# Gating sixteen modulation pieces on the gMLP's gated products

## The chip, the cores and the metric

The kernel runs as one program on one NeuronCore of a Trainium2 chip. The metric is the device time of one execution in microseconds (us), as the median of several runs. The engines are TensorE (PE, matmuls), VectorE (DVE), ScalarE (ACT), GpSimd (POOL) and SyncE (SP), which here issues DMAs.

## What is computed

Two trunk layers over 512 latent tokens of width 1024 with 256 context tokens, one sample, fp32. Layer 0 mixes tokens by windowed attention, layer 1 by a chunked gMLP; a routed mixture of experts (MoE) with 16 experts, two per token, follows each. Around every mixer stands a modulation that is computed from the conditioning vector. Cut to what matters here (layer 1):

```python
mod_l = silu(c) @ w_mod[i] + b_mod[i]          # six rows of 1024: shift, scale, gate of mixer and of MoE
hl = x * (1 + sc_a) + sh_a
z = gelu(hl @ w_in + b_in); u, v = z[..., :1024], z[..., 1024:]
v = layer_norm(v, ln_g, ln_b)                  # over the width
s = einsum("gpq,bnqgc->bnpgc", w_s, v) + b_s   # chunks of 128 tokens, 8 groups of 128 columns
yl = (u * s) @ w_out
x = layer_norm(ALPHA * x + g_a * yl, ln1_g, ln1_b)
hl = x * (1 + sc_f) + sh_f                     # input of the router and the experts
x = layer_norm(ALPHA * x + g_f * moe(hl), ln2_g, ln2_b)
```

## The kernel before

**Modulation pieces.** Layer 1's product `silu(c) @ w_mod[1]` is computed without TensorE. `w_mod` comes from HBM in pieces `("mt", 1, j)`, j from 0 to 47, each a 128x1024 tile holding 128 outputs on its partitions. `gemt(1, j)` multiplies such a tile by the broadcast row `srow[0]` (the activated c, stored in HBM as `sdr`) and sums along the row into one column of `mv[1]`. For the pieces 32 to 47 an odd j is done by VectorE in one instruction (line 361, product and sum), an even j by GpSimd (line 363, the product, in place) and ScalarE (line 364, the sum). After every eighth j small VectorE steps (lines 370, 372) finish eight columns, and for some a TensorE transpose and a DMA write them out as a row. The columns 24 to 47 are wanted by the router's matrices (lines 761 to 777 in `ln1_rows`) and by the second MoE.

**The weight stream.** All weight tiles stand in one list, `pieces`, in the order in which SyncE issues their DMAs into the buffers `raw`. `adv(...)` marks a piece as used and lets the stream run on: `LR[0]` loads and `LS[0]` splits ahead of it. A split (lines 226, 227) turns a weight tile into a high part `wh` on ScalarE and the remainder `wl` on VectorE, so that fp32 products are made of three matmuls in a faster format: high by high, low by high, high by low.

**The gMLP.** It comes after layer 0's MoE. First v is projected for four token tiles (`vhalf`), its statistics taken (line 646, 651) and it is normalised (`vnorm`: a chain of small VectorE steps `cny`, `cnv`, `cnu`, lines 734 to 746, the mean term `cnm` at line 656, and then ScalarE at line 1360). The last of the four tiles has its statistics only when the u loop starts. The u loop (`for f in range(8)`) is the place of the change. One iteration f projects u for 128 columns over all tokens (24 matmuls, lines 1399 to 1401, of which the third is the first that needs `wl`), runs `gemt` for two pieces, applies gelu to u on ScalarE (`uT`, line 1406), makes the gate matmuls (line 1409, eight instructions, two per token tile of v), and on VectorE scales and adds the bias (`sg`, line 1412) and multiplies by `uT` (1415). The product is split for the output projection: ScalarE casts the high half (1417), VectorE subtracts it (1418, the low half, `gp[:, 1]`, which the change names `lo`). `mix_out(1, "wout", ...)` then multiplies all eight gated tiles by `wout` (lines 792 to 794), with the small router matmuls of lines 768 and 771 between.

**What sets the order.** The Python code issues instructions to a Tile scheduler, which simulates a timeline and fixes each engine's instruction order; waits go by semaphores. Code order, dependencies and buffer counts therefore all bear on where an instruction stands on its engine, and each engine runs its list strictly in order.

Of the kernel before, what the change touches and what calls it, by code (L numbers as in the profile page):

```python
# [8 lines left out]
F32 = mybir.dt.float32  # L9
# [4 lines left out]
OP = mybir.AluOpType  # L14
# [87 lines left out]
def hybrid_kernel(ctx: ExitStack, tc: tile.TileContext, A, out):  # L102
    nc = tc.nc
    V, SC, PE, GP, SP = nc.vector, nc.scalar, nc.tensor, nc.gpsimd, nc.sync
# [14 lines left out]
    def slot(shape, dt=F32, nm="s"):  # L119
        return S.tile(shape, dt, name=f"{nm}{nid()}", tag="s")  # L120
# [7 lines left out]
    def hslot(shape, dt=F32, nm="h"):  # L128
        return PP[0].tile(shape, dt, name=f"{nm}{nid()}", tag="h")
# [7 lines left out]
    def psB():  # L137
        return ps.tile([128, 512], F32, name=f"pb{nid()}", tag="B", bufs=2)

    def psT(dt=F32):  # L140
        return ps.tile([128, 512], dt, name=f"pt{nid()}", tag="T", bufs=2)

    def small(shape, dt=F32, nm="m", bufs=2):
        return sm.tile(shape, dt, name=f"{nm}_{nid()}", tag=nm, bufs=bufs)

    def tt2(shape, dt=F32, nm="t"):
        return sm.tile(shape, dt, name=f"{nm}_{nid()}", tag="t2", bufs=9)
# [3 lines left out]
    pieces = [("mod", 0, j) for j in range(16)]  # L151
# [10 lines left out]
    def moe_pieces(l):  # L162

        r, us = [], UNITS[l]

        def use(v, js):
            r.extend(p for p in [("moe", l, v, j) for j in js] if p not in r)
        for i, (v, o, n, row) in enumerate(us):
            use(v, range(8))
            if i:  # L170
                use(us[i - 1][0], range(8, 12))
            if i == 1:
                use(v, range(8, 12))
        use(us[-1][0], range(8, 12))
        return r

    pieces += moe_pieces(0)
    pieces += [("winv", j) for j in range(8)] + [("ws",)]
    for j in range(8):
        pieces += [("winu", j), ("mt", 1, 32 + 2 * j), ("mt", 1, 33 + 2 * j)]  # L180
    pieces += [("wout", j) for j in range(8)]
    pieces += moe_pieces(1)
    pos = {p: i for i, p in enumerate(pieces)}
# [3 lines left out]
    LS, LR = [4], [8]  # L187
# [57 lines left out]
    def raw(*p):  # L245
        i = pos[p]
        used.add(i)
        issue(i + 1)
        return raws[p]

    def hl(*p):
        ensure_split(pos[p] + 1)
        return pairs[p]

    def adv(*p):
        i = pos[p]
        issue(i + 1 + LR[0])
        ensure_split(i + 1 + LS[0])
        issue(i + 1 + LS[0] + LR[0])
# [55 lines left out]
    sdr = dr.tile([1, D], F32, name="sdr")  # L315
# [10 lines left out]
    mv = [cst.tile([128, 48], F32, name=f"mv{l}") for l in range(2)]  # L326
# [28 lines left out]
        if n >= 2:  # L355
            V.tensor_scalar(m, m, 1.0, None, op0=OP.add)

    def gemt(l, j):
        w = raw("mt", l, j)
        if (j % 4 != 3 if l and j < 32 else j % 2):  # L360
            V.scalar_tensor_tensor(w, w, 1.0, srow[0], op0=OP.mult, op1=OP.mult, accum_out=mv[l][:, j:j + 1])  # L361
        else:
            GP.tensor_mul(w, w, srow[0])  # L363
            SC.activation(w, w, AF.Identity, accum_out=mv[l][:, j:j + 1])
        adv("mt", l, j)
        if j % 8 < 7:
            return
        i = j // 8
        m = mv[l][:, i * 8:i * 8 + 8]
        V.tensor_add(m, m, bcol[:, l, i * 8:i * 8 + 8])  # L370
        if i in (1, 4):
            V.tensor_scalar(m, m, 1.0, None, op0=OP.add)
        if i >= 2:
            q = psT()
            PE.transpose(q[0:8, 0:128], m, idf)
            r = tt2([8, 128], F32, "gr")
            SC.copy(r, q[0:8, 0:128])
            SC.dma_start(mdr[l * 4 + i - 2].rearrange("(a b) -> a b", b=128), r)

    def load_row(ap, nm="row", alloc=slot, q=SC):  # L380
        t = alloc([128, D], F32, nm)
        q.dma_start(t, ap.to_broadcast([128, D]))
        return t

    LS[0], LR[0] = 4, 14
    srow = []
# [18 lines left out]
    for a in range(2):  # L405
        cr = raw("cT", a)
        hi, lo = slot([128, 4, 256], F32R, "cTh"), slot([128, 4, 256], F32R, "cTl")
# [6 lines left out]
    for a in range(4):  # L414
        xr = raw("xT", a)
        hi, lo = hslot([128, 2, 512], F32R, "hTh"), hslot([128, 2, 512], F32R, "hTl")
# [158 lines left out]
    def after(i, b, c=mybir.DependencyClass.NoSync):  # L575
        tc.add_manual_dep(i.ins, b.ins.name, mybir.DependencyInfo(
            c, mybir.DependencyReason.DATA), reason="order")
# [71 lines left out]
    def ln_rstd(st, w):  # L649
        mv = small([128, 2], F32, w + "mv")  # L650
        V.bn_aggr(mv, st)
        v = small([128, 3], F32, w + "nv")
        V.tensor_scalar(v[:, 0:1], mv[:, 1:2], EPS, None, op0=OP.add)
        y = newton([v[:, i:i + 1] for i in range(3)], w)
        nmr = small([128, 1], F32, w + "nm")
        V.scalar_tensor_tensor(nmr, mv[:, 0:1], -1.0, y, op0=OP.mult, op1=OP.mult)
        return y, nmr
# [607 lines left out]
    def mix_out(l, name, X, lh):  # L1265
        ga, g1, b1 = ln1_rows(l)
        for j in range(8):
            hl(name, j)
        LS[0], LR[0] = 0, 8
        s = small([128, 4, 16], F32, "rs", 1)  # L1270
        lg = psB()[:, 0:64]
        st = small([128, 4, 2, 6], F32, "ast", 1)
        for n in range(2):
            for t in range(4):
                f = out_half(l, name, n, lh, X[t], ga, t, lg)
                V.bn_stats(st[:, t, n, :], X[t][:, n * 512:(n + 1) * 512])
                f()
                if n:
                    x = X[t]
                    rstd, nmr = ln_rstd(st[:, t], "a")  # L1280

                    def sig(t=t, rstd=rstd, nmr=nmr):
                        R = RT[l]
                        u = small([128, 16], F32, "ru")
                        V.scalar_tensor_tensor(u, R["se"], nmr, R["be"], op0=OP.mult, op1=OP.add)
                        V.scalar_tensor_tensor(u, lg[:, t * 16:(t + 1) * 16], rstd, u, op0=OP.mult, op1=OP.add)
                        return SC.activation(s[:, t, :], u, AF.Sigmoid)
                    with tc.issue_after(sig().ins):
                        SC.activation(x, x, AF.Identity, bias=nmr, scale=rstd)
                        SC.dma_start(hdr[t * 128:(t + 1) * 128, :], x)  # L1290
            adv(name, 4 * n + 3)
        issue(pos["moe", l, 2, 0])
        RT[l]["s"] = s
        route(l, s)

        def rest(t0, t1):
            for t in range(t0, t1):
                V.tensor_mul(X[t], X[t], g1)
                V.tensor_add(X[t], X[t], b1)
        return rest  # L1300
# [4 lines left out]
    rest = mix_out(0, "wo", X0, lambda t, c, s: OT[t, c // 4][:, s, (c % 4) * 128:(c % 4 + 1) * 128])  # L1305
    py, gf = moe(0, rest, X0)
    binv = load_row(A["binv"], alloc=uslot)


    X = X0  # L1310
# [77 lines left out]
    for f in range(8):  # L1388
        fs = slice(f * 128, f * 128 + 128)
        V.scalar_tensor_tensor(bs[:, fs], p[:, fs], gcol[:, 8 + f:9 + f], bsr[:, fs], op0=OP.mult, op1=OP.add)  # L1390
    LS[0], LR[0] = 2, 4
    srow[0] = load_row(sdr, alloc=uslot)
    gated = []
    for f in range(8):
        wh, wl = hl("winu", f)
        p = psB()
        for k in range(8):
            ws = slice(k * 128, k * 128 + 128)
            PE.matmul(p, wh[:, ws], gk[k][0], start=(k == 0), stop=False)
            PE.matmul(p, wh[:, ws], gk[k][1], start=False, stop=False)  # L1400
            PE.matmul(p, wl[:, ws], gk[k][0], start=False, stop=(k == 7))
        for j in range(2):
            gemt(1, 32 + 2 * f + j)
        adv("winu", f)
        uT = tt2([128, 512], F32, "uT")
        SC.activation(uT, p, AF.Gelu_apprx_tanh, bias=binu[:, f:f + 1])
        p = psT()
        for t in range(4):
            PE.matmul(p[:, t * 128:(t + 1) * 128], vv[t][:, f * 128:(f + 1) * 128],
                      wsr[:, f * 128:(f + 1) * 128], start=(t == 0), stop=(t == 3), skip_group_check=True)  # L1410
        tm = tt2([128, 512], F32, "sg")
        V.scalar_tensor_tensor(tm.rearrange("p (t n) -> p t n", t=4), p.rearrange("p (t n) -> p t n", t=4),
                               gcol[:, f:f + 1], bs[:, None, f * 128:(f + 1) * 128].to_broadcast([128, 4, 128]),
                               op0=OP.mult, op1=OP.add)
        V.tensor_mul(tm, tm, uT)
        gp = slot([128, 2, 512], F32R, "gp")
        SC.copy(gp[:, 0, :], tm)
        V.tensor_sub(gp[:, 1, :], tm, gp[:, 0, :].bitcast(F32))
        gated.append(gp)
    rest = mix_out(1, "wout", X, lambda t, c, s: gated[c][:, s, t * 128:(t + 1) * 128])  # L1420
    py, gf = moe(1, rest, X)
    g2 = load_row(A["ln2_g"][1:2, :])
# [68 lines left out]
```

## Time and profile before

| | |
|---|---|
| median of 3 runs | 1204.68 us (1203.26 to 1208.51) |
| the profiled execution | 1204.38 us |
| its span in the trace | 1202.6 us (1.8 us lie around it) |
| mean granted TensorE clock | 0.932 of full speed |
| TensorE busy | 1040.9 us, 87% of the span |
| VectorE busy | 619.2 us, 51% |
| ScalarE busy | 357.4 us, 30% |
| GpSimd busy | 263.4 us, 22% |

The u loop lies at about 740 to 809 us of the span, the output projection behind it until about 842. All times in rows are counted from the span's start. A row of the timeline gives start, duration, engine, line of the kernel, operation, output and inputs, count of instructions merged, and in brackets how long the engine stood idle before and who released it.

### The profile page before, as it was taken

What the parts mean: (1) busy time and instruction counts of PE and PEld (TensorE: products, weight loads), DVE (VectorE), ACT (ScalarE), POOL (GpSimd) and SP (SyncE); (2) the same over time, 40 slices, a digit from 0 to 9 for tenths busy, and PEclk for the clock granted to TensorE, in tenths of its full rate; (3) what the DMA queues carried; (4) which work ended last, traced back from release to release, by engine and by line L of the source; (5) the groups of instructions that cost most, each with busy time, mean ns of one, the idle gap of its engine ahead of it and who ended that gap; (6) DMA issues with size and microseconds to landing.
All of it is one profiled execution on the core that took longest, in us unless ns stands there. A gap on an engine that the chain in (4) does not pass through costs nothing. (4 is left out here: it accounts for less than half of the span.)

```text
span 1202.6 us, 17652 instructions
## 1 busy us (share of the span) xinstructions
PE 1040.9 (87%) x6216; PEld 593.4 (49%) x6216; DVE 619.2 (51%) x1532; ACT 357.4 (30%) x724; POOL 263.4 (22%) x245
## 2 busy tenths in 40 slices
PE   6889898986995989999998589699859899999980
PEld 2567665553783334444443368488723344433420
DVE  1799999785357612221113987875674221221147
ACT  1553587774312101111111343352211111111103
POOL 0044243323000113231003242410011121211131
PEclk9999899997996989999999799799969899999995
DMA  8945467546376979999998116466589993999981
GB/s 332 404 152 181 142 210 245 175 154 229 109 270 248 393 289 355 410 410 410 410 409 323 78 60 240 141 204 235 183 298 411 360 410 144 365 410 409 411 321 70
DMA packets 103672, 330.96 MB, mean 275 GB/s; under 512 B 13057, under 2 KB 23761, under 8 KB 103570
## 3 DMA queue, kind: packets, MB, share of 16 engines
q1 hardware_dynamic: 88336, 287.43, 63.1%
q0 software_dynamic: 10512, 27.28, 6.1%
q10 hardware_dynamic: 4722, 14.98, 3.6%
q8 instruction: 53, 0.87, 0.3%
q14 instruction: 49, 0.40, 0.1%
HBM read 310.72 MB, written 22.07 MB: 277 GB/s over the span
## 5 line engine op out<-in xcount | busy, mean ns | idle before, releaser
L1035 PE MATMUL pb<-ring,xt 128*32 128x256 f32 (+1 forms) x1824 | 225.1, 467 | 12.4 <-DVEq L1257 11.6
L1035 PEld LDWEIGHTS pb<-ring,xt 128*32 128x32 f32 (+1 forms) x1824 | 83.5, 121 | 130.9 <-issue 89.0
L1046 DVE TENSOR_TENSOR si<-si,pb 128x256 f32<-128x256 f32 (+1 forms) x43 | 15.7, 365 | 213.8 <-ACT si L1045 213.8
L1079 POOL DMA_DIRECT2D ydr<-ys x114 | 58.1, 516 | 298.0 <-DVE ys L1074 245.9
L363 POOL TENSOR_TENSOR raw<-raw,row 128x1024 f32<-128x1024 f32 x32 | 91.5, 2873 | 129.0 <-ACT kh L476 55.9
L1068 PE MATMUL pb<-ring,hh 128*32 128x256 f32 (+1 forms) x912 | 114.4, 462 | 0.5 <-ACT hh L1057 0.5
L361 DVE SCALAR_TENSOR_TENSOR raw<-raw,row 128x1024 f32<-128x1024 f32 x48 | 87.5, 1841 | 3.1 <-DMA row<-sdr 3.1
L1045 ACT ACTIVATE si<-pb 128x256 f32<-128x256 f32 (+1 forms) x43 | 14.6, 339 | 233.6 <-PE pb L1035 233.6
L1035 PE MATMUL pa<-ring,xt 128*128 128x512 f32 x160 | 72.9, 601 | 0.0
L1068 PEld LDWEIGHTS pb<-ring,hh 128*32 128x32 f32 (+1 forms) x912 | 39.8, 119 | 58.5 <-issue 42.4
L998 POOL DMA_INDIRECT xg<-hdr,Rgi x22 | 23.4, 1063 | 185.3 <-DVE pq L870 147.9
L227 DVE TENSOR_TENSOR wl<-raw,wh 128x1024 fp32r<-128x1024 f32 x44 | 55.8, 1296 | 13.4 <-ACT wh L226 13.4
L562 DVE TENSOR_SCALAR_CACHE_REDUCE P<-pa,nsink 128x512 f32<-128x512 f32 (+1 forms) x64 | 50.6, 810 | 19.7 <-PE pa L558 9.8
L1057 ACT COPY hh<-pt 128x256 f32<-128x256 f32 (+2 forms) x48 | 17.0, 354 | 146.2 <-PE pt L1055 146.2
L1074 DVE TENSOR_TENSOR ys<-pb,gfs 128x512 f32<-128x512 f32 (+1 forms) x39 | 22.1, 567 | 60.0 <-PE pb L1068 60.0
L564 ACT ACTIVATE P<-P,nm 128x512 f32<-128x512 f32 (+1 forms) x64 | 49.4, 773 | 11.9 <-DVE P L562 11.6
L1015 ACT ACTIVATE xt<-pt,bc,gc 128x128 f32<-128x128 f32 x88 | 33.1, 456 | 59.5 <-PE pb L967 35.5
L1035 PEld LDWEIGHTS pa<-ring,xt 128*128 128x128 f32 x160 | 28.9, 190 | 39.2 <-issue 39.2
L598 ACT COPY PT<-pt 128x512 f32<-128x512 f32 x72 | 39.4, 580 | 28.7 <-PE pt L597 28.6
L597 PE MATMUL pt<-cc,P 128*128 128x128 f32 x288 | 44.1, 282 | 4.1 <-ACT PT L598 3.5
L226 ACT CAST wh<-raw 128x1024 fp32r<-128x1024 f32 x44 | 44.4, 1044 | 10.4 <-DMA mdr<-gr 7.7
L597 PEld LDWEIGHTS pt<-cc,P 128*128 128x128 f32 x288 | 31.2, 142 | 31.7 <-issue 25.8
(366 smaller groups left out, 2043.1 us busy)
## 6 DMA issues: line engine op xcount, KB each, us to landing
ring<-in_moe SPq DMA_DIRECT2D x336, 512.0 KB, 10.6
raw<-in_mt SPq DMA_DIRECT2D x80, 512.0 KB, 4.8
raw<-in_moe SPq DMA_DIRECT2D x48, 512.0 KB, 6.8
raw<-in_mod SPq DMA_DIRECT2D x16, 512.0 KB, 10.2
raw<-in_qkv SPq DMA_DIRECT2D x12, 512.0 KB, 10.2
ydr<-ys POOLq DMA_DIRECT2D x42, 128.0 KB, 5.4
ydr<-zero SPq DMA_DIRECT2D x10, 512.0 KB, 6.2
raw<-in_wo SPq DMA_DIRECT2D x8, 512.0 KB
```

Source lines behind the costliest of these rows:

```text
L226: SC.copy(hi, src)
L227: V.tensor_sub(lo, src, hi.bitcast(F32))
L361: V.scalar_tensor_tensor(w, w, 1.0, srow[0], op0=OP.mult, op1=OP.mult, accum_out=mv[l][:, j:j + 1])
L363: GP.tensor_mul(w, w, srow[0])
L562: V.tensor_scalar(P[j], reg, -0.125, nsink[:, p * 8 + j:p * 8 + j + 1], op0=OP.mult, op1=OP.min, accum_out=nm[:, j:j + 1])
L564: SC.activation(P[j], P[j], AF.Exp, bias=nm[:, j:j + 1], scale=-1.0, accum_out=sums[:, j:j + 1])
L597: PE.transpose(pt[:, j * 128:(j + 1) * 128], P[a * 4 + j][:, i * 128:(i + 1) * 128], idf)
L598: cp = SC.copy(tl[:, a, :], pt)
L1015: SC.activation(o, i, AF.Identity, bias=b, scale=g)
L1035: PE.matmul(o.rearrange("p (m c) -> p m c", m=2), xt[:, k, c:c + n], w[:, h], start=(k == 0), stop=(k == 7), skip_group_check=True)
L1068: PE.matmul(o, ht[f], w[:, h], start=(f == 0), stop=(f == 3), skip_group_check=True)
L1079: GP.dma_start(ydr[row:row + n, h * n * 8:(h + 1) * n * 8], ys[h * n:h * n + n, :])
```

## The change

Four edits. (1) In the list of pieces each u weight stands one iteration earlier: the first ahead of all, and the next before the two modulation pieces of each iteration. (2) `gemt` takes a third argument; its first instruction, on VectorE or GpSimd, gets a dependency on it. (3) In the u loop `gemt` is called at the iteration's end, with the subtraction that makes the low half as that argument; the stream's lookahead is 3 splits and 6 loads instead of 2 and 4. (4) The row `sdr` is fetched at the end of layer 0's MoE instead of just before the loop.

```diff
     pieces += [("winv", j) for j in range(8)] + [("ws",)]
+    pieces += [("winu", 0)]
     for j in range(8):
-        pieces += [("winu", j), ("mt", 1, 32 + 2 * j), ("mt", 1, 33 + 2 * j)]
+        pieces += [("winu", j + 1)] * (j < 7) + [("mt", 1, 32 + 2 * j), ("mt", 1, 33 + 2 * j)]
...
-    def gemt(l, j):
+    def gemt(l, j, past=None):
         w = raw("mt", l, j)
         if (j % 4 != 3 if l and j < 32 else j % 2):
-            V.scalar_tensor_tensor(w, w, 1.0, srow[0], op0=OP.mult, op1=OP.mult, accum_out=mv[l][:, j:j + 1])
+            first = V.scalar_tensor_tensor(w, w, 1.0, srow[0], op0=OP.mult, op1=OP.mult, accum_out=mv[l][:, j:j + 1])
         else:
-            GP.tensor_mul(w, w, srow[0])
+            first = GP.tensor_mul(w, w, srow[0])
+        if past:
+            after(first, past, mybir.DependencyClass.Sync)
+        if not (j % 4 != 3 if l and j < 32 else j % 2):
             SC.activation(w, w, AF.Identity, accum_out=mv[l][:, j:j + 1])
...
     binv = load_row(A["binv"], alloc=uslot)
+    srow[0] = load_row(sdr, alloc=uslot)
...
-    LS[0], LR[0] = 2, 4
-    srow[0] = load_row(sdr, alloc=uslot)
+    LS[0], LR[0] = 3, 6
...
-        for j in range(2):
-            gemt(1, 32 + 2 * f + j)
         adv("winu", f)
...
-        V.tensor_sub(gp[:, 1, :], tm, gp[:, 0, :].bitcast(F32))
+        lo = V.tensor_sub(gp[:, 1, :], tm, gp[:, 0, :].bitcast(F32))
         gated.append(gp)
+        for j in range(2):
+            gemt(1, 32 + 2 * f + j, lo)
```

Line numbers of the changed kernel run ahead of those before: 227 becomes 228, 361 becomes 362, 363 becomes 364, 364 becomes 368, 656 becomes 660, 768 becomes 772, 793 becomes 797, 1360 becomes 1365, 1409 becomes 1411, 1412 becomes 1414, 1418 becomes 1420.

On VectorE, ahead of the loop, where the last v tile's variance (`cmv`, `cnv`) is done and its Newton steps (`cny`) follow, before:

```order
L651 BN_AGGR cmv_7062<-cst_7059 128x2
L653 TENSOR_SCALAR cnv_7064<-cmv_7062 128x1
L361 SCALAR_TENSOR_TENSOR raw_6880,mv_141<-raw_6880,row_7096 128x1024
L361 SCALAR_TENSOR_TENSOR raw_7133,mv_141<-raw_7133,row_7096 128x1024
L361 SCALAR_TENSOR_TENSOR raw_7144,mv_141<-raw_7144,row_7096 128x1024
L734 TENSOR_SCALAR cny_7066<-cnv_7064 128x1
L735 TENSOR_SCALAR cnv_7064<-cnv_7064 128x1
```

and of the change:

```order
L655 BN_AGGR cmv_7064<-cst_7061 128x2
L657 TENSOR_SCALAR cnv_7066<-cmv_7064 128x1
L738 TENSOR_SCALAR cny_7068<-cnv_7066 128x1
L739 TENSOR_SCALAR cnv_7066<-cnv_7066 128x1
L741 TENSOR_SCALAR cnv_7066<-cnv_7066 128x1
```

The three products on modulation tiles (`raw` by `row`) that stood between the variance and the Newton steps are gone from there.

On VectorE in the first two iterations of the loop (`sg` to `gp` the gating, `wl` the low part of a coming u weight), before:

```order
L1412 SCALAR_TENSOR_TENSOR sg_7153<-pt_7148,cols,bs_7087 128x512
L1412 SCALAR_TENSOR_TENSOR sg_7204<-pt_7199,cols,bs_7087 128x512
L1415 TENSOR_TENSOR sg_7153<-sg_7153,uT_7146 128x512
L1415 TENSOR_TENSOR sg_7204<-sg_7204,uT_7197 128x512
L1418 TENSOR_TENSOR gp_7156<-sg_7153,gp_7156 128x512
L227 TENSOR_TENSOR wl_7192<-raw_7135,wh_7191 128x1024
L1418 TENSOR_TENSOR gp_7207<-sg_7204,gp_7207 128x512
L227 TENSOR_TENSOR wl_7243<-raw_7186,wh_7242 128x1024
L361 SCALAR_TENSOR_TENSOR raw_7195,mv_141<-raw_7195,row_7096 128x1024
```

and of the change:

```order
L1414 SCALAR_TENSOR_TENSOR sg_7152<-pt_7147,cols,bs_7089 128x512
L1414 SCALAR_TENSOR_TENSOR sg_7203<-pt_7198,cols,bs_7089 128x512
L1417 TENSOR_TENSOR sg_7152<-sg_7152,uT_7145 128x512
L1417 TENSOR_TENSOR sg_7203<-sg_7203,uT_7196 128x512
L1420 TENSOR_TENSOR gp_7155<-sg_7152,gp_7155 128x512
L362 SCALAR_TENSOR_TENSOR raw_7127,mv_141<-raw_7127,row_6488 128x1024
L228 TENSOR_TENSOR wl_7166<-raw_7129,wh_7165 128x1024
L1420 TENSOR_TENSOR gp_7206<-sg_7203,gp_7206 128x512
L362 SCALAR_TENSOR_TENSOR raw_7133,mv_141<-raw_7133,row_6488 128x1024
L228 TENSOR_TENSOR wl_7217<-raw_7139,wh_7216 128x1024
```

Each `wl` stands behind the `gp` of an iteration and the modulation product gated by it. GpSimd's products, one per iteration, keep their order on that engine and wait for the same `gp`.

On VectorE at the loop's end, where the `wl` of the output projection's first two weight tiles are made (the two in a row), before:

```order
L1412 SCALAR_TENSOR_TENSOR sg_7466<-pt_7461,cols,bs_7087 128x512
L1415 TENSOR_TENSOR sg_7466<-sg_7466,uT_7459 128x512
L1418 TENSOR_TENSOR gp_7469<-sg_7466,gp_7469 128x512
L227 TENSOR_TENSOR wl_7505<-raw_7448,wh_7504 128x1024
L227 TENSOR_TENSOR wl_7509<-raw_7450,wh_7508 128x1024
L1412 SCALAR_TENSOR_TENSOR sg_7527<-pt_7522,cols,bs_7087 128x512
L1415 TENSOR_TENSOR sg_7527<-sg_7527,uT_7520 128x512
```

and of the change:

```order
L1414 SCALAR_TENSOR_TENSOR sg_7512<-pt_7507,cols,bs_7089 128x512
L1417 TENSOR_TENSOR sg_7512<-sg_7512,uT_7505 128x512
L1420 TENSOR_TENSOR gp_7515<-sg_7512,gp_7515 128x512
L362 SCALAR_TENSOR_TENSOR raw_7373,mv_141<-raw_7373,row_6488 128x1024
L228 TENSOR_TENSOR wl_7524<-raw_7380,wh_7523 128x1024
L228 TENSOR_TENSOR wl_7528<-raw_7422,wh_7527 128x1024
```

These two stood ahead of the last iteration's `sg`; now they stand behind the last iteration's `gp` and its modulation product.

## Rows read from the trace of the kernel before

**Rows 1.** Windows: us, busy us (count) per engine, clock, DMA share, GB/s

```profile
752.30:763.00 10.70, 0.06 (x1) 0.00 (x0) 9.06 (x14) 1.26 (x2) 8.30 (x4) 0.62 0.24 83
763.00:772.00 9.00, 7.74 (x22) 5.75 (x23) 7.66 (x12) 7.75 (x13) 0.00 (x0) 0.50 0.63 186
790.00:810.00 20.00, 20.00 (x107) 17.04 (x106) 14.31 (x18) 10.02 (x15) 2.84 (x1) 1.00 0.67 220
36.35:45.00 8.65, 4.31 (x10) 2.98 (x11) 8.26 (x19) 7.41 (x11) 0.00 (x0) 1.00 1.03 410
657.86:661.69 3.83, 0.00 (x1) 0.00 (x1) 3.83 (x5) 0.00 (x0) 3.52 (x2) 1.00 1.03 420
661.69:665.00 3.31, 3.31 (x10) 1.47 (x12) 3.31 (x3) 0.00 (x0) 0.14 (x1) 0.65 1.02 417
```

**Rows 2.** Timeline, TensorE: start us, duration us, operation, [idle before, releaser]

```profile
751.53 0.83 PE L1409 MATMUL pt<-raw,v 128*128 128x128 f32 x6
...
763.03 1.22 PE L1409 MATMUL pt<-raw,v 128*128 128x128 f32 x4 [10.67 <-ACT v L1360]
```

**Rows 3.** Timeline, ScalarE, two operations in the same stretch

```profile
748.49 1.06 ACT L757 ACTIVATE row<-row 128x1024 f32<-128x1024 f32 x1 [2.23 <-DMA row<-in_ln_g]
...
761.74 1.24 ACT L1360 ACTIVATE v<-v,cnm,cny 128x1024 f32<-128x1024 f32 x1 [10.19 <-DVE cnm L656]
```

**Rows 4.** Timeline, VectorE, before the loop

```profile
742.69 0.15 DVE L653 TENSOR_SCALAR cnv<-cmv 128x1 f32<-128x1 f32 x1
...
745.92 1.23 DVE L361 SCALAR_TENSOR_TENSOR raw<-raw,row 128x1024 f32<-128x1024 f32 x1 [3.07 <-DMA row<-sdr]
...
747.07 3.42 DVE L361 SCALAR_TENSOR_TENSOR raw<-raw,row 128x1024 f32<-128x1024 f32 x1
...
754.11 1.92 DVE L741 SCALAR_TENSOR_TENSOR cnu<-cny,cnv 128x1 f32<-128x1 f32 x1
...
758.35 2.26 DVE L741 SCALAR_TENSOR_TENSOR cnu<-cny,cnv 128x1 f32<-128x1 f32 x1
...
761.48 0.16 DVE L656 SCALAR_TENSOR_TENSOR cnm<-cmv,cny 128x1 f32<-128x1 f32 x1
```

**Rows 5.** Timeline, VectorE: ends of an undisturbed Newton chain

```profile
844.34 0.15 DVE L734 TENSOR_SCALAR any<-anv 128x1 int32<-128x1 int32 x1
...
846.25 0.16 DVE L656 SCALAR_TENSOR_TENSOR anm<-amv,any 128x1 f32<-128x1 f32 x1
```

**Rows 6.** Timeline, GpSimd, the five products before the loop

```profile
746.03 14.57 POOL L363 TENSOR_TENSOR raw<-raw,row 128x1024 f32<-128x1024 f32 x5 [2.48 <-DMA row<-sdr]
```

**Rows 7.** Timeline, VectorE, in the loop

```profile
763.86 1.41 DVE L1412 SCALAR_TENSOR_TENSOR sg<-pt,cols,bs 128x512 f32<-128x512 f32 x2 [2.22 <-PE pt L1409]
...
772.53 2.36 DVE L763 TENSOR_TENSOR bc<-bc,mv 128x8 f32<-128x8 f32 x1
...
776.80 0.69 DVE L1415 TENSOR_TENSOR sg<-sg,uT 128x512 f32<-128x512 f32 x1
...
778.18 0.69 DVE L1418 TENSOR_TENSOR gp<-sg,gp 128x512 fp32r<-128x512 f32 x1 [0.69 <-ACT gp L1417]
...
782.00 0.75 DVE L1412 SCALAR_TENSOR_TENSOR sg<-pt,cols,bs 128x512 f32<-128x512 f32 x1 [1.64 <-PE pt L1409]
...
807.44 1.23 DVE L227 TENSOR_TENSOR wl<-raw,wh 128x1024 fp32r<-128x1024 f32 x1 [2.04 <-ACT wh L226]
```

**Rows 8.** Timeline, TensorE: gate matmuls, router matmuls, first mix_out matmul with wl

```profile
780.91 1.06 PE L1409 MATMUL pt<-raw,v 128*128 128x128 f32 x8
...
807.40 1.86 PE L768 MATMUL pt<-rwg,onesf 128*128 128x16 f32 x16
...
809.11 0.49 PE L792 MATMUL pa<-wh,gp 128*128 128x512 f32 x1
...
809.43 0.40 PE L793 MATMUL pa<-wl,gp 128*128 128x512 f32 x1
```

**Rows 9.** Line 363, GpSimd's products; ns: least, median, most

```profile
L363 POOL TENSOR_TENSOR raw<-raw,row x8: 2332/2665/3375, 746.0 to 791.1; 128x1024 f32<-128x1024 f32 x8
```

## Prediction

> **What bounds the kernel now.** I read the windows of the stage first, then the timelines of TensorE, ScalarE, VectorE and GpSimd beside one another, and last GpSimd's products by form. The stage is the gMLP's u loop. TensorE is full over most of it (20.00 of 20 us in 790 to 810), but between 752.3 and 763 it does 0.06 us of work, and it runs at half clock for the 9 us behind [rows 1]. The hole is one wait: behind the gate matmuls at 751.53 the next start at 763.03, after 10.67 us, released by ScalarE's norm of v at line 1360 [rows 2]. That norm starts at 761.74 after 10.19 us of waiting for VectorE's `cnm` [rows 3]. VectorE has the variance at 742.84 (742.69 + 0.15), yet `cnm` only at 761.64 [rows 4]: the three modulation products of line 361 and then the short Newton steps stand in between, each stretched. A product takes 1.23 us at first and then 3.42 (the third likewise), and a 128x1 step 1.92 to 2.26, where the whole chain of such steps takes 2.07 us elsewhere (844.34 to 846.41) [rows 4, 5]. All this time GpSimd runs five products, 746.03 to 760.60 [rows 6]; the last stretched step ends at 760.61, together with GpSimd's last product. A VectorE operation with two SBUF inputs and a GpSimd product do not run together here, and they take turns: five GpSimd and three VectorE products alternate.
>
> **What goes: 11.2 us.** Without the products ahead of it `cnm` is ready at 742.84 + 2.07 = 744.9. On ScalarE the norm stands behind the scaling of a layer-norm row (line 757 of before), which starts at 748.49 because its row lands then [rows 3], and behind one gelu (0.69): 748.49 + 1.06 + 0.69 + 1.24 = 751.5 at the latest. So the gate matmuls follow those of 751.53 with no wait. From a full set of them to `sg` takes 1.09 us (780.91 to 782.00) [rows 7, 8], hence the first `sg` at 752.62, where before had 763.86 [rows 7]: −11.24.
>
> **What comes back in the loop.** Before, three VectorE and five GpSimd products were done in the hole; now all sixteen stand in the loop, each pair behind its iteration's `lo`. On VectorE the next u weight's `wl` (line 228 of after) is queued behind the gated product, and TensorE's third matmul of a projection waits for that `wl`. I take VectorE's two-input operations and GpSimd's products as one resource, from the first `sg` on, by the rows: `sg`, multiply and `lo` together 2.13 (0.75 + 0.69 + 0.69), a VectorE product 1.15 (from the start of one to that of the next, 745.92 to 747.07), a `wl` of the same size likewise, a GpSimd product 2.33 (the least of the eight; the median of 2.67 holds turns that it waited) [rows 4, 7, 9].
> - Before, from 763.86 to the end of the second wout `wl` at 808.67 [rows 7]: 7 x 2.13 + 8 `wl` x 1.15 + 5 products x 1.15 + 3 x 2.33 + 1.3 of small steps = 38.2. That stretch took 44.8, so 6.6 stood idle, waiting for TensorE.
> - After, to the end of the first wout `wl`, which the new order puts last: 8 x 2.13 + 7 x 1.15 + 8 x 1.15 + 8 x 2.33 + 1.3 = 54.2.
>
> With nothing idle that `wl` would end at 752.62 + 54.2 = 806.8, with before's idle at 813.4. Between these ends I place it by what must be exposed in each iteration: between multiply and `lo` ScalarE casts the high half, and VectorE sits idle 0.69 (from 776.80 + 0.69 to 778.18) [rows 7]; nothing else that is ready stands there in the new order. 8 x 0.69 = 5.5, so 812.3.
>
> **The end of the loop: +4.7.** Before, mix_out came in right behind TensorE's other work: the router's 16 small matmuls (line 768) at 807.40, its own first at 809.11, and line 793, the first that needs a `wl`, at 809.43 [rows 8]; two wout `wl` were done by then. After, line 797 waits for the first of them, to about 812.4: +3.0 (from −2.5 with 806.9 to +4.1 with 813.5). And the 16 matmuls, 1.7 us that lay ahead of mix_out, now stand inside it. Together +4.7 on the path (bounds −0.8 and +5.8), the 11.2 won already in it. Beyond that the routing and the second MoE follow mix_out's end one for one.
>
> **The clock: +2.** The hole cost a second time before: 9 us at 0.50 of the clock [rows 1]. After, TensorE has several holes: from 752.4 until the third projection's `wl` is there, 752.62 + 2 x 0.75 + 3 x 0.69 + 1.15 + 2.33 + 1.15 = 760.8, broken only by that projection's first two matmuls; smaller ones in later iterations; and one before mix_out, whose `wl` comes two iterations of VectorE's work behind that of the last projection. The trace has both answers to such a hole: one of 4.30 us left the clock at 1.00 (36.35 to 45.00), one of 3.83 was followed by 3.31 us at 0.65 [rows 1]. The loss of the second is 0.35 x 3.31 = 1.2 us, that of before's large hole at most 0.50 x 9 = 4.5. I take one of the size of 2, with bounds of 0 and 7.
>
> **The other edits at nothing.** The row `sdr` is fetched earlier, at the end of the first MoE, where DMA is full (share 1.03 at 657.86 to 661.69 [rows 1]): 512 KB at 420 GB/s is 1.25 us if it delays something, and as much is taken out of 738 to 752; −1.3 to +1.3. The u weights come one piece earlier and 6 loads and 3 splits run ahead instead of 4 and 2: DMA's share is 0.24 in the hole [rows 1], so what is needed first has long landed. A gated piece holds its buffer longer; if that starved the stream, wout would come late, but its casts now wait for VectorE anyway.
>
> Sum on the profiled execution: 1204.38 + 4.7 + 2 = 1211.1; its time lies 0.3 below the median of the runs, so 1211.4.
>
> **A rule against the row.** Rows 4 and 6 show strict turns: whichever of the two waits gets the next slot. The Trainium skill, SBUF — State Buffer, section "Who interferes with whom", says that whoever issues first gets the shared pair for the whole instruction and that the other is fully blocked. It names no turn for the one that waits. By that alone a VectorE that always has its next operation ready could pass a waiting GpSimd again and again, the products would end off the path, and the time would be that of the first rival; by the row each product of GpSimd is paid once per iteration.
>
> **Rivals.**
> 1. *The stall goes and the products hide (faster).* GpSimd's 8 products run while VectorE does `sg` (PSUM input) or waits; those of before behind 772 stretched only some VectorE operations (2.36 at 772.53 [rows 7]). Then the loop keeps before's time, 763.86 to 809.43 or 45.6: mix_out's line 797 at 798.2, −11.2, with +1.7 for the router −9.5: 1195.2. Against it: only three GpSimd products lay in that stretch, and VectorE had waits for TensorE in between (1.64 before 782.00), 6.6 us of idle time in all; five more products of 2.33 don't fit into that.
> 2. *Gain and give-back cancel (same).* VectorE and GpSimd have next to no idle time, the wout `wl` ends at 806.8 to 810, and no hole is long enough for the clock: −0.8 to +2.5, about 1205.5. For it: the casts can lie beside a GpSimd product. Against it: on VectorE `lo` comes behind its own cast and the products behind `lo`, so only another iteration's work could fill the time of the cast.
> 3. *The clock decides (much slower).* Each hole from the third iteration on halves the clock as before's did; once slow, a projection (5.5 us) takes up to 4.5 more, and the chain `lo`, product, product, `wl`, projection closes over it. It decides from holes longer than 4.3 us on: +4.7 + 7, which is 1216.4.
>
> **How the numbers follow.** Forecast 0.40, its own range 1207.5 to 1215 (+3 to +10.5); rival 1 0.24; rival 2 0.26; rival 3 0.10. This kernel's runs can tell about 0.5%, 6 us, from no change. Slower by more: 0.33 of the forecast's 0.40, and rival 3's 0.10: 0.43. Within: the rest of the forecast, 0.07, and rival 2's 0.26: 0.33. Faster: rival 1, 0.24. Rival 1 spreads from 1191 to 1199 (its loop may also win back part of the slow clock of before's first projections), rival 3 up to 1220; the range leaves out the lower part of the one and the upper of the other: 1194 to 1218.
>
> **What would show it.** Right: TensorE goes from the gate matmuls of the second iteration on without the 10.67 us; `cnm` ready near 745; Newton steps of 0.16 to 0.22; then in each iteration `lo`, a VectorE product of 1.2, a GpSimd product of 2.3 beginning as that ends, and a `wl` of 2.3 or more that ends with or behind it; TensorE waiting for VectorE at line 1405; first wout `wl` near 812. Wrong: projections of the loop back to back, `wl` at 1.23 beside running GpSimd products, or mix_out starting before 806. The clock term is wrong if the granted clock stays at 1.00 from 752 to 815.

## The result: 0.9% slower

The changed kernel takes 1213.74 us (median of 6 runs, 1212.7 to 1217.46) against 1203.71 us (6 runs, 1203.09 to 1208.51): ratio 1.0088, with an interval of 1.0068 to 1.0108, or some 8 to 13 us. The forecast was +6.7 us. The two profiled executions differ by 8.3 us (1210.9 against 1202.6 us of span). The stage starts 0.65 us earlier in this one (the first `bs` of line 1395 at 739.75, before at 740.40); the times below can be held against those of before with that shift.

The stall is gone. VectorE's timeline of the changed kernel, from the last variance to the second `wl` of the loop:

```profile
742.05 0.15 DVE L657 TENSOR_SCALAR cnv<-cmv 128x1 f32<-128x1 f32 x1
...
744.14 0.16 DVE L660 SCALAR_TENSOR_TENSOR cnm<-cmv,cny 128x1 f32<-128x1 f32 x1
751.97 1.41 DVE L1414 SCALAR_TENSOR_TENSOR sg<-pt,cols,bs 128x512 f32<-128x512 f32 x2 [7.67 <-PE pt L1411]
...
754.66 0.69 DVE L1420 TENSOR_TENSOR gp<-sg,gp 128x512 fp32r<-128x512 f32 x1
755.39 1.23 DVE L362 SCALAR_TENSOR_TENSOR raw<-raw,row 128x1024 f32<-128x1024 f32 x1
...
756.54 3.35 DVE L228 TENSOR_TENSOR wl<-raw,wh 128x1024 fp32r<-128x1024 f32 x1
759.82 0.68 DVE L1420 TENSOR_TENSOR gp<-sg,gp 128x512 fp32r<-128x512 f32 x1
760.53 1.22 DVE L362 SCALAR_TENSOR_TENSOR raw<-raw,row 128x1024 f32<-128x1024 f32 x1
...
761.85 3.23 DVE L228 TENSOR_TENSOR wl<-raw,wh 128x1024 fp32r<-128x1024 f32 x1
```

`cnm` is done at 744.30 (forecast 744.9) and the first `sg` starts at 751.97 instead of 763.86 [rows 7], 11.2 us earlier once the shift is taken off. Behind each `gp` (line 1420, the gate) comes the VectorE product at its undisturbed 1.23 us, and then a `wl` of 3.35 or 3.23 that takes 1.23 elsewhere [rows 7]. What it waits for is seen on GpSimd:

```profile
755.44 3.38 POOL L364 TENSOR_TENSOR raw<-raw,row 128x1024 f32<-128x1024 f32 x1 [12.53 <-DVE gp L1420]
760.58 3.42 POOL L364 TENSOR_TENSOR raw<-raw,row 128x1024 f32<-128x1024 f32 x1 [1.76 <-DVE gp L1420]
```

The product starts with VectorE's and takes 3.38, that is VectorE's 1.15 and then its own 2.2 to 2.3; it ends at 758.82, and the `wl` behind it 1.07 later. All eight of GpSimd's products in the loop look so (3.38 to 3.44), and five of them stretch a `wl`. TensorE pays for it (idle time and releaser in brackets):

```profile
755.63 0.50 PE L1403 MATMUL pb<-gh,wh 128*128 128x512 f32 x1 [0.80 <-ACT wh L227]
...
759.95 0.80 PE L1405 MATMUL pb<-gh,wl 128*128 128x512 f32 x1 [3.58 <-DVE wl L228]
...
774.19 0.50 PE L1405 MATMUL pb<-gh,wl 128*128 128x512 f32 x1 [1.51 <-DVE wl L228]
```

The other three products reach the loop another way. ScalarE sums each of them (line 368), and what it casts next stands behind that sum in its list. In the fifth iteration nothing on VectorE is stretched: `sg`, which reads its first input from PSUM, takes its 0.75 beside the running product, and the `wl` its 1.23, but late (rows of four engines' timelines, in order of time):

```profile
785.98 3.43 POOL L364 TENSOR_TENSOR raw<-raw,row 128x1024 f32<-128x1024 f32 x1 [6.29 <-DVE gp L1420]
787.09 0.75 DVE L1414 SCALAR_TENSOR_TENSOR sg<-pt,cols,bs 128x512 f32<-128x512 f32 x1
789.44 1.06 ACT L368 ACTIVATE raw<-raw 128x1024 f32<-128x1024 f32 x1 [4.27 <-POOL raw L364]
790.50 1.03 ACT L227 CAST wh<-raw 128x1024 fp32r<-128x1024 f32 x1
791.56 1.23 DVE L228 TENSOR_TENSOR wl<-raw,wh 128x1024 fp32r<-128x1024 f32 x1 [3.72 <-ACT wh L227]
791.58 0.50 PE L1403 MATMUL pb<-gh,wh 128*128 128x512 f32 x1 [0.84 <-ACT wh L227]
```

In the fourth, VectorE's steps on the finished columns wait 3.46 us for ScalarE's sum, and a TensorE transpose (line 379) waits 1.92 for them; in the seventh, ScalarE's cast of the gated product stands behind the sum. At the start of mix_out, with the router's matmuls of line 772 behind:

```profile
808.44 1.22 PE L796 MATMUL pa<-wh,gp 128*128 128x512 f32 x2 [3.68 <-ACT wh L227]
812.77 0.79 PE L797 MATMUL pa<-wl,gp 128*128 128x512 f32 x1 [3.11 <-DVE wl L228]
...
821.24 1.86 PE L772 MATMUL pt<-rwg,onesf 128*128 128x16 f32 x16
```

Line 797, the first of mix_out that needs a `wl`, starts at 812.77 (forecast 812.4; before 809.43 [rows 8]) after waits of 3.68 for `wh` and 3.11 for `wl`, and the 16 router matmuls of line 772 are inside mix_out now. The windows have the clock (us, busy us (count) of TensorE, its weight loads, VectorE, ScalarE, GpSimd, then granted clock, DMA share and GB/s):

```profile
752.00:760.00 8.00, 2.99 (x21) 2.21 (x19) 7.88 (x9) 3.52 (x6) 3.38 (x1) 0.98 0.38 126
760.00:764.00 4.00, 4.00 (x11) 3.20 (x12) 3.88 (x4) 1.05 (x1) 3.42 (x1) 0.61 0.44 131
764.00:790.00 26.00, 22.57 (x112) 18.38 (x112) 15.71 (x25) 9.99 (x16) 10.19 (x4) 1.00 0.51 162
790.00:808.40 18.40, 12.49 (x55) 9.32 (x53) 12.71 (x15) 9.33 (x16) 7.01 (x3) 0.98 0.84 286
808.40:818.00 9.60, 6.45 (x15) 4.62 (x16) 9.60 (x9) 7.85 (x9) 3.24 (x1) 0.51 0.00 0
```

Before, the 9 us behind the stall ran at 0.50 [rows 1]. Now only 4 us there are slow (0.61), and a second slow stretch lies at the start of mix_out: 0.51 over 808.4 to 818, where a matmul comes every 0.43 us, later every 0.23. TensorE stands idle 17.5 of the stage's 73.0 us, before 11.9 of 69.0.

### The profile page after: what moved, and what is told of

Read it like the earlier page. It is cut to its first block, busy times and chain, and to the rows that moved or that the text cites. A ratio compares the mean times of both kernels' runs of the same rounds, so it can differ in the third digit from the quotient of the medians.

```text
span 1210.9 us, 17661 instructions
## 1 busy us (share of the span) xinstructions
PE 1042.6 (86%) x6216; PEld 593.0 (49%) x6216; DVE 614.0 (51%) x1532; ACT 357.9 (30%) x724; POOL 270.2 (22%) x245
## 5 line engine op out<-in xcount | busy, mean ns | idle before, releaser
L364 POOL TENSOR_TENSOR raw<-raw,row 128x1024 f32<-128x1024 f32 x32 | 99.1, 3112 | 138.0 <-DMA raw<-in_mt 69.9
L362 DVE SCALAR_TENSOR_TENSOR raw<-raw,row 128x1024 f32<-128x1024 f32 x48 | 81.2, 1708 | 0.3
L228 DVE TENSOR_TENSOR wl<-raw,wh 128x1024 fp32r<-128x1024 f32 x44 | 61.5, 1431 | 12.7 <-ACT wh L227 11.7
L568 ACT ACTIVATE P<-P,nm 128x512 f32<-128x512 f32 (+1 forms) x64 | 49.4, 773 | 11.8 <-DVE P L566 11.4
L1021 DVE TENSOR_SCALAR xt<-pt,gc,bc 128x128 f32<-128x128 f32 x88 | 30.1, 402 | 37.8 <-PE pt L1013 37.7
```

The lines of the kernel that those rows point to most:

```text
L228: V.tensor_sub(lo, src, hi.bitcast(F32))
L362: first = V.scalar_tensor_tensor(w, w, 1.0, srow[0], op0=OP.mult, op1=OP.mult, accum_out=mv[l][:, j:j + 1])
L364: first = GP.tensor_mul(w, w, srow[0])
L568: SC.activation(P[j], P[j], AF.Exp, bias=nm[:, j:j + 1], scale=-1.0, accum_out=sums[:, j:j + 1])
```

## The experiments

Two theories were held against each other. The first: VectorE's operations with two SBUF inputs and GpSimd's products take turns, so what decides is where a product stands in VectorE's order and how long a turn it takes. The second: the cost lies in something else, as the gate itself, the amount of work, or the stream of weights. In the table "stage" goes from the first `bs` to the first mix_out matmul that needs a `wl`, in the profiled execution; the ratio is to the kernel before, run on the same chip.

| kernel | ratio (interval) | first `sg` | first `wl` matmul of mix_out | stage, us |
|---|---|---|---|---|
| before | 1 | 763.86 | 809.43 | 69.0 |
| the change | 1.0088 (1.0068 to 1.0108) | 751.97 | 812.77 | 73.0 |
| e1_norm_first | 0.9947 (0.9925 to 0.9969) | 752.59 | 803.47 | 64.7 |
| e2_late | 0.9992 (0.9977 to 1.0007) | 751.73 | 806.39 | 66.9 |
| e3_all_dve | 1.0024 (1.0008 to 1.0041) | 751.60 | 804.97 | 65.6 |
| e4_pool_free | 1.0018 (1.0004 to 1.0032) | 747.35 | 801.75 | 66.2 |
| e5_norm_first_dve | 0.9885 (0.986 to 0.991) | 747.22 | 793.44 | 58.8 |
| e6_hybrid | 0.9947 (0.9928 to 0.9966) | 747.89 | 796.68 | 60.6 |
| e7_tail | 1.0031 (1.0018 to 1.0043) | 753.36 | 811.06 | 69.9 |
| e8_old_stream | 1.0458 (1.0433 to 1.0482) | 749.85 | 861.54 | 123.6 |
| e9_old_ahead | 1.0095 (1.0064 to 1.0126) | 750.68 | 813.28 | 74.4 |
| e10_all_pool | 1.0139 (1.011 to 1.0168) | 755.96 | 819.60 | 75.9 |
| e11_row_only | 0.9945 (0.9926 to 0.9964) | 754.62 | 798.62 | 54.7 |
| e12_dve_row | 0.993 (0.9902 to 0.9958) | 751.52 | 797.13 | 57.4 |

The profiled executions reach the stage at 734.6 to 743.9, so single times of two kernels can't be compared directly, the stages can.

**e1_norm_first: the stall alone.** The kernel before; `vn` is the last `cnm`.

```diff
-            gemt(1, 32 + 2 * f + j)
+            gemt(1, 32 + 2 * f + j, vn)
```

> The kernel before with one edit: the products of the loop's sixteen modulation pieces wait for the last v norm's cnm (so they stand behind the Newton steps) and for nothing else; stream, row fetch and their place in the code stay as before. Theory (VectorE and GpSimd take turns, and where a product stands in VectorE's order decides): cnm is ready near 745, the three VectorE and five GpSimd products run between 745 and 758, the first sg comes near 753.5 instead of 763.9, and the loop behind it keeps its pace: 1193 to 1198 us, 6 to 10 under before. Rival (what the stall costs is given back later whatever is done, since the products have to be done somewhere): within 3 us of before.

0.9947, some 6 us faster: the theory holds, and the rival falls. The stage shrinks by only 4.4 us, though the first `sg` comes 9.7 earlier, counted from the first `bs`. Against what was expected, the loop did not keep its pace (50.9 us from the first `sg` to mix_out instead of 45.6), since GpSimd's five products run from 744.85 to 760.40 beside its first operations:

```profile
753.38 1.16 PE L1414 MATMUL pt<-raw,v 128*128 128x128 f32 x8 [2.18 <-DVE sg L1417]
757.56 0.80 PE L1404 MATMUL pb<-gh,wh 128*128 128x512 f32 x1 [3.01 <-ACT wh L226]
...
762.13 0.79 PE L1406 MATMUL pb<-gh,wl 128*128 128x512 f32 x1 [3.35 <-DVE wl L227]
```

TensorE waits 2.2, 3.0 and 3.35 us there, where before it waited once for 10.67 [rows 2].

**e2_late: the same work behind the `wl`.** The changed kernel with the pair gated by the `wl` of the weight two iterations on (`raw` and `hl` only let the stream run that far; the seventh pair stays as it was).

```diff
+        for j in range(2):
+            raw("mt", 1, 32 + 2 * f + j)
+        if f != 6:
+            ahead = ("winu", f + 2) if f < 6 else ("wout", 0)
+            hl(*ahead)
+            lo = wlop[ahead]
```

> The changed kernel with the sixteen products gated by the wl of the weight two iterations on (the first wl of wout for the last pair; the seventh pair as in the change) instead of by lo: the same work on the same engines, only each product pair stands behind the wl and not ahead of it. Theory: wl comes 3.4 us earlier after lo, TensorE's waits at line 1405 go, the first mix_out matmul with wl at 803 to 808 instead of 812.8: 1203 to 1208 us. Rival (the gating itself, buffers held and sums late, or the amount of work in the loop): as the change or slower, 1213 or more.

0.9992, 10 to 12 us better than the change with the same products on the same engines, all still gated; the gate itself is not what costs. VectorE, at the place of the rows above:

```profile
755.37 1.23 DVE L231 TENSOR_TENSOR wl<-raw,wh 128x1024 fp32r<-128x1024 f32 x1 [0.26 <-ACT wh L230]
756.63 1.23 DVE L366 SCALAR_TENSOR_TENSOR raw<-raw,row 128x1024 f32<-128x1024 f32 x1
...
757.78 2.87 DVE L1424 TENSOR_TENSOR gp<-sg,gp 128x512 fp32r<-128x512 f32 x1
760.58 1.21 DVE L231 TENSOR_TENSOR wl<-raw,wh 128x1024 fp32r<-128x1024 f32 x1
```

The `wl` is back at 1.23, and the one that is stretched is the next iteration's `gp` (2.87 instead of 0.69): the turn is paid later, where more of it is hidden. TensorE's longest wait at line 1409, the third matmul there, is 0.86. What is left is one wait of 6.53 for the first `wh` of wout, ahead of mix_out.

**e3_all_dve and e10_all_pool: the size of a turn.** All sixteen products on VectorE, or all on GpSimd, in the changed kernel.

```diff
-        if (j % 4 != 3 if l and j < 32 else j % 2):
+        if (j % 4 != 3 if l and j < 32 else j % 2 or l):          # e3_all_dve
+        if (j % 4 != 3 if l and j < 32 else j % 2 and not l):     # e10_all_pool
```

> The changed kernel with all sixteen products of the loop on VectorE (line 362's form), GpSimd and ScalarE doing none; gate and places as in the change. Theory (a GpSimd product takes 2.33 us of the shared resource and a VectorE product 1.15): the resource's work falls by 8 x (2.33 - 1.15) = 9.4 us, the mix_out matmul with wl comes at 802 to 805 instead of 812.8: 1202 to 1205 us. Rival (VectorE's own load counts, not the turns): 8 x 1.15 = 9.2 us more on VectorE, 1218 to 1222.

> The changed kernel with all sixteen products of the loop on GpSimd (line 364's form, summed by ScalarE). Theory (turns; a GpSimd product costs 2.33 of the shared resource, a VectorE product 1.15): 8 x 1.18 = 9.4 us more of the resource, mix_out's first matmul with wl at 820 to 825 instead of 812.8, 1220 to 1226 us. Rival (VectorE's load binds, GpSimd's work is beside it): 8 x 1.15 = 9.2 us less on VectorE, 1203 to 1208.

More work on VectorE makes the stage 7.4 us shorter, less of it makes it 2.8 longer (ratios 1.0024 and 1.0139 against 1.0088; both times lie about at the edge of what was expected), so VectorE's load does not bind. That it is the length of the turn and nothing else is not shown. e3 takes away ScalarE's eight sums too: TensorE waits 10.8 us in its stage instead of 17.5, and of the 6.7 less only 3.3 are waits for `wl`; 1.4 are waits for `wh`, and 1.9 the transpose that waits for ScalarE's sum. In e10 TensorE waits no longer than in the change (16.9 us); it is busy longer with the same 258 matmuls (58.9 us instead of 55.5), at a clock of 0.83 over 765 to 772 and 788 to 798 and 0.79 over 798 to 806.

Nor does work add up to time. By the prediction's sum the shared resource has 44.8 us of work in e3, 54.2 in the change and 63.6 in e10; from the first `sg` to mix_out's first `wl` matmul they took 53.4, 60.8 and 63.6. That e10's 63.6 us of work took just 63.6 is chance: VectorE stands idle for 9.2, 16.2 and 25.6 us of these times, and GpSimd's products run in part beside `sg` or in that idle time. With all on VectorE each product takes its 1.15 and the `wl` is undisturbed:

```profile
755.02 1.23 DVE L362 SCALAR_TENSOR_TENSOR raw<-raw,row 128x1024 f32<-128x1024 f32 x1
...
756.17 1.22 DVE L362 SCALAR_TENSOR_TENSOR raw<-raw,row 128x1024 f32<-128x1024 f32 x1
...
757.31 1.22 DVE L228 TENSOR_TENSOR wl<-raw,wh 128x1024 fp32r<-128x1024 f32 x1
```

**e4_pool_free: GpSimd's products ungated.**

```diff
-        if past:
+        if past and j % 2:
```

> The changed kernel with GpSimd's eight products ungated (they run when their piece has landed); VectorE's eight stay gated by lo. Theory: GpSimd's first products fall between 742 and 758 again and stretch some Newton steps, but not by VectorE products: the first sg 0 to 3 us later than in the change; in the loop GpSimd seldom stands between lo and wl: mix_out at 804 to 809, 1203 to 1209 us. Rival (gating of VectorE's own products is what costs): 1211 to 1214.

As the theory has it (1.0018), except that no Newton step was stretched: from the first `bs` to the first `sg` it takes 11.8 us, the change 12.2. GpSimd's products still meet VectorE's (the first gated one takes 3.27 us at 750.78), but four of the eight ran ahead of the first `sg` (718.96 to 742.91), and the others seldom fall between `lo` and `wl`.

**e5_norm_first_dve: both together.** e1_norm_first with e3's condition.

> The kernel before with the loop's products behind the last cnm, as in e1_norm_first, and besides all sixteen on VectorE. Theory (a GpSimd product takes 2.33 us of the shared resource, a VectorE product 1.15): six products fit between cnm and the first sg, the second wl after it is no longer held by GpSimd's five products, and the loop has 8 x 1.18 us less of the resource; mix_out at 797 to 800 instead of 803.5: 1188 to 1194 us. Rival (the resource is no longer what binds once the stall is gone; TensorE is): as e1, within 2 us of it. Second rival (VectorE's load): slower than e1.

0.9885, 11 to 17 us faster than the kernel before and the fastest of all. Six products fit between `cnm` and the first `sg`, and TensorE waits for little:

```profile
748.02 1.16 PE L1414 MATMUL pt<-raw,v 128*128 128x128 f32 x8 [0.97 <-DVE sg L1417]
750.87 0.80 PE L1404 MATMUL pb<-gh,wh 128*128 128x512 f32 x1 [1.69 <-ACT wh L226]
```

and the window of the loop behind these waits (columns as above):

```profile
752.00:793.40 41.40, 41.37 (x202) 34.83 (x202) 31.76 (x52) 13.61 (x20) 0.00 (x0) 0.94 0.60 193
```

TensorE is busy in 41.37 of the loop's last 41.4 us: here it binds at last, and the rival (e1's time again) falls. Its clock is 0.50 from 752 to 756, behind these two waits, and 1.00 from 758 on. Like e3, this kernel has none of the loop's sums on ScalarE, so its gain over e1 is not that of the shorter turn alone.

**e6_hybrid: only the first four pieces ahead of the loop.** e1_norm_first, with pieces 36 to 47 behind the fourth u weight's `wl`.

```diff
+        if f >= 2:
+            hl("winu", 3)
+            past = wlop["winu", 3]
```

> As e1_norm_first, but only the pieces of the first two iterations run freely behind cnm; the others wait for the wl of the fourth u weight, so that no product stands between the first lo and the first two wl. Theory: TensorE's waits of 3.0 and 3.4 us before the third projection shrink to about 1 us each, as in e2_late; two products on each engine move into the loop (7 us of the resource, part of it in idle time): mix_out at 800 to 804, 1192 to 1197 us. Rival (work moved into the loop is paid in full): 1199 to 1203.

The stage is 4.1 us shorter than in e1, but the ratio is the same 0.9947, and the time lies between what the theory and the rival had. TensorE's two waits are 2.29 and 0.53, and a new one of 2.59 is that of the transpose. Behind mix_out's start this execution takes 4.9 us longer than e1's until the experts' first gather (76.3 against 71.4). The router's two groups of 16 small matmuls come back to back there, and behind them the clock falls, though TensorE never stands idle:

```profile
801.15 2.87 PE L779 MATMUL pt<-cols,bc 128*128 128x16 f32 x16
803.86 0.77 PE L801 MATMUL pa<-wl,gp 128*128 128x512 f32 x1
```

It is 0.66 over 801.1 to 803.8 and 0.52 until 809. The first group lay ahead of mix_out in e1 (1.7 us), the second took 1.7 there and takes 2.7 here, and the eleven matmuls behind it take 4.84 instead of 2.5: together the 4.9.

**e7_tail: the end of the loop.** The last pair behind the second `wl` of wout.

```diff
+        if f == 7:
+            raw("mt", 1, 46)
+            raw("mt", 1, 47)
+            hl("wout", 1)
+            lo = wlop["wout", 1]
```

> The changed kernel with the last iteration's two products behind the second wl of wout instead of behind lo. Theory: the first wl of wout comes 3.4 us earlier (809.4 instead of 812.8), and the hole before mix_out shrinks so that its clock falls for a shorter time: 1208 to 1211 us. Rival (the end is bound by the stream of wout or by ScalarE's casts): no change, 1213 to 1215.

1.0031, some 7 us under the change, a little more than expected: the `wl` no longer waits for a GpSimd product, and TensorE's second wait is gone.

```profile
809.80 1.22 PE L800 MATMUL pa<-wh,gp 128*128 128x512 f32 x2 [3.67 <-ACT wh L230]
811.06 0.79 PE L801 MATMUL pa<-wl,gp 128*128 128x512 f32 x1
```

**e8_old_stream and e9_old_ahead: the weight stream.** The changed kernel with the old order of pieces and the old lookahead, and with the old lookahead alone.

```diff
-    pieces += [("winu", 0)]
-        pieces += [("winu", j + 1)] * (j < 7) + [("mt", 1, 32 + 2 * j), ("mt", 1, 33 + 2 * j)]
+        pieces += [("winu", j), ("mt", 1, 32 + 2 * j), ("mt", 1, 33 + 2 * j)]      # e8 only
-    LS[0], LR[0] = 3, 6
+    LS[0], LR[0] = 2, 4                                                            # e8 and e9
```

> The changed kernel with the weight stream of before: the u weights in their old place and 2 splits and 4 loads ahead; gate, places and the early row stay. Theory (that edit costs and gains nothing by itself): within 3 us of the change, 1211 to 1217. Rival (the earlier u weights are part of what moved the time): if they helped, 1220 or more, as each wl then waits for its load; if they hurt, 1208 or less.

> The changed kernel with 2 splits and 4 loads ahead instead of 3 and 6; the u weights keep their new place in the stream. Theory (in e8_old_stream each u weight lay behind a gated pair in the stream, and the order of the pieces, not the lookahead, closed that loop): TensorE has no waits of 3 us for wh in each iteration, 1211 to 1218 us. Rival (the number of loads ahead is what the gated pieces use up): 1235 or more.

e8 is far outside what the theory had, on the side of the rival in which the earlier u weights help: 1.0458, 55 us slower than before, 44 slower than the change. e9 is the change again (1.0095), so it is the order, at least with the old lookahead (the old order with the new one wasn't tried). With it the weight's DMA stands behind those of a gated pair in SyncE's queue (start, duration of the issue and its waits):

```profile
743.12 14.55 SPq L210 DMA_DIRECT2D raw<-in_mt  x2
757.76 0.38 SPq L210 DMA_DIRECT2D raw<-in_winu  x1
```

The pair's issues take 14.55 us, nearly all of it waits, and the u weight goes out only then. In the change a pair's issues take 13.24 there (from 737.93), but the u weight has gone out ahead of them, at 737.51. SyncE's waits over e8's loop end mostly on TensorE's line 1404 (43.3 us), VectorE's `wl` (22.3) and its products (17.0); that they are for buffers which the gated pieces hold is argued from the code. TensorE waits for `wh` and `wl` in every iteration, with 14 to 16 us from one to the next:

```profile
767.75 0.50 PE L1402 MATMUL pb<-gh,wh 128*128 128x512 f32 x1 [2.21 <-ACT wh L226]
...
772.07 0.80 PE L1404 MATMUL pb<-gh,wl 128*128 128x512 f32 x1 [3.58 <-DVE wl L227]
```

**e11_row_only and e12_dve_row: the early row.** The row's fetch at its new place, in the kernel before and in e5_norm_first_dve.

```diff
+    srow[0] = load_row(sdr, alloc=uslot)     # behind binv
-    srow[0] = load_row(sdr, alloc=uslot)     # before the loop
```

> The kernel before with the one edit that sdr's row is fetched at the end of the first MoE; stream, places and no gate as before. Its first products then stand ahead of the last v norm in another place: they run as their pieces land, and none stands between the last variance and its Newton steps. Theory (the stall is the products' place in VectorE's order): most of the 10.7 us stall goes, GpSimd's products still stretch some steps: 1193 to 1199 us. Rival (products must be gated to stay off the norm): 1201 to 1205.

> As e5_norm_first_dve, with sdr's row fetched early too. Theory: the six products ahead of the loop no longer wait for the row (1.1 us there), TensorE's waits of 1.0 and 1.7 us shrink: 0 to 2 us under e5_norm_first_dve, ratio to before 0.986 to 0.989. Rival: nothing, since TensorE binds there.

The row alone is worth 0.9945 without any gate. The products run as their pieces land, between the norms of the earlier v tiles:

```profile
725.98 1.20 DVE L361 SCALAR_TENSOR_TENSOR raw<-raw,row 128x1024 f32<-128x1024 f32 x1
...
740.22 1.22 DVE L361 SCALAR_TENSOR_TENSOR raw<-raw,row 128x1024 f32<-128x1024 f32 x1
```

and GpSimd's first:

```profile
721.96 2.41 POOL L363 TENSOR_TENSOR raw<-raw,row 128x1024 f32<-128x1024 f32 x1 [11.02 <-DMA raw<-in_mt]
```

The stage begins later for it (743.93) and is 14.3 us shorter than before. The last `cnm` still comes only at 752.54, as two of its steps take 2.25 and 2.34 beside two GpSimd products (747.06 to 751.85); but the first `sg` stands at 754.62, 10.7 us behind the first `bs`, where before it was 23.5. On top of e5 it gave nothing that the ratios show: 0.993 (0.9902 to 0.9958), where 0.986 to 0.989 was expected and e5 has 0.9885 (0.986 to 0.991), on different chips, though the stage itself is 1.4 us shorter. Whether the early row costs ahead of the stage was not settled.

## Why the prediction was right, and where it wasn't

- *The stall goes, 11.2 us.* Right to the tenth; e1 shows that it is worth having.
- *What comes back in the loop.* The mechanism is right: a product of GpSimd and VectorE's operations with two SBUF inputs take turns, and a turn between `lo` and `wl` is paid. e2 shows that it is the place that costs. The strict turns held wherever a GpSimd product waited beside a VectorE one (3.38 to 3.44 in all eight cases). What the Trainium skill says in SBUF — State Buffer, "Who interferes with whom", that the other is blocked for the whole instruction, agrees with these rows. That a waiting one could be passed over, the reading on which the first rival stood, did not happen in the loop.
- *The sum of the loop.* It put mix_out's first `wl` matmul at 812.4; it came at 812.77, or 813.4 with the shift. That close a hit is partly luck, since the terms are not those of the trace. The sum has 54.2 us of one resource and 5.5 of idle time. In the trace VectorE is busy 44.6 of the 60.8 us (its waits for GpSimd's turns are in this) and idle 16.2; `sg`, which the sum put on the resource, runs beside GpSimd; only five of the eight turns stretch a `wl`, and the other three come through ScalarE's sums, which the prediction did not have. Before's loop was worked out the same way: VectorE stood idle 10.7 of its 44.8 us (34.1 busy), not 6.6.
- *The end of the loop, +4.7.* Right in its parts (+3.3, or +4.0 by the length of the stage, and 1.7). e7 takes most of it back.
- *The clock, +2: too small, and one of its two rows was misread.* Half clock shows twice: 0.61 over 760 to 764, some 1.6 us that are already in the time of mix_out's start, and 0.51 at the start of mix_out, where the 12 matmuls from 812.77 to 817.92 take 5.15 us and would take 2.7 at a pitch of 0.23: 2.4. From mix_out's first `wl` matmul to the experts' first gather the change takes 76.15 us and the kernel before 71.68 (881.11 less 809.43): 4.5 more, of which those 2.4 and the router's 1.7 are 4.1. 3.3 + 4.5 = 7.8 is the shift at that gather (888.92), and 8.3 at the end of the span. The other 1.7 us to the 10.0 between the medians are where the two profiled executions lie among their runs: that of the change 1.0 below its median, that of before 0.7 above.
- *The hole of 4.30 us.* The prediction took it as one that left the clock at 1.00. The row says so, but the matmuls behind the hole came at the pace that goes with 0.50 elsewhere in the same trace, five in 2 us; from 46 to 48 there are eleven. In the change's trace the same stretch, 36.85 to 46, has 0.50. So the third rival's limit of 4.3 us had no row under it.

```profile
42.00:44.00 2.00, 2.00 (x5) 1.61 (x6) 2.00 (x4) 2.00 (x4) 0.00 (x0) 1.00 1.03 410
92.00:94.00 2.00, 2.00 (x5) 1.61 (x6) 2.00 (x2) 1.43 (x4) 1.57 (x2) 0.50 0.14 27
```

- *The other edits at nothing.* The sum does not contradict it, but the reason was wrong. That "what is needed first has long landed" was read from DMA's share in the hole. But the share says nothing of a queue in which a load waits for a buffer: with the gate, the order of the pieces is worth 44 us (e8). And the early row gains 6 to 7 us by itself in the kernel before (e11); in the change the gate holds back the products that it would let run.
- *The rivals.* The first fell in the change, though part of it was there: of GpSimd's 27.2 us in the loop 2.3 lay beside `sg` and 5.8 in VectorE's idle time. Its time (1195) is near the 1197 that e1 and e11 reach, by other ways. The second had VectorE and GpSimd with next to no idle time; VectorE stood idle 16.2 of the 60.8 us, and both together 10.5. The third, clock holes from the third iteration on, fell: between 764 and 808.4 the clock stayed at 0.98 to 1.00, with holes of up to 1.9 us ahead of the one before mix_out.

## What to carry to other kernels

Where two engines take turns on a resource, a wait that is removed by moving their work has to be costed by where each turn lands next: behind the operation that the bottleneck waits for, most of it is hidden; ahead of it, it stretches that operation (here in five iterations of eight). Look also at who works on the moved result: in the other three the turn came back through ScalarE's queue. When a short chain stands behind long independent work on an in-order engine, gate that work on the chain's end and not on each later iteration, and give the work to the engine with the shorter turn even if that engine is the busier one (e5: 0.9885, where it also took the sums off ScalarE). A gate also holds buffers: look at what stands behind the gated load in its queue.

## What the runs showed that was not expected

Profiled executions of kernels whose code is the same up to the stage reach it some us apart (739.75 in the change, 743.74 in e10_all_pool). The length of a hole alone does not tell what the clock does. In the changed kernel's stage it fell to half with the hole of 4.4 us (0.80 and 3.58, two matmuls between) and with that of 3.68 ahead of mix_out, and stayed up through those of 1.9 us and less. But in e5 it was half behind waits of 0.97 and 1.69, and in e6 behind 32 small matmuls with no hole at all.
